# Down projection of a SwiGLU block on one Trainium2 core: 16 of its 44 feature tiles by Strassen pairs

## The chip, the cores and the metric

The kernel runs on one core of one Trainium2 chip. The metric is the device time of one execution in microseconds (us), as the median of several runs. A core has five engines that run their own instruction lists in order and wait for one another by semaphores: TensorE (PE in the profile; its weight loads are PEld), VectorE (DVE), ScalarE (ACT), GpSimd (POOL) and SyncE (SP). SP, ACT and POOL also issue DMA transfers, each on its own queue. The matmuls take float32 numbers split into a high and a low part, so that one exact-enough product is three matmuls: high by low, high by high, low by high.

## The reference, cut to what matters

```python
def reference(x, ..., ffn_pre_g, ffn_post_g, w_gate_up, w_down):
    ...                                   # attention and convolution give h (512 x 2048)
    u = rms_norm(h, ffn_pre_g[l])
    gate, up = jnp.split(u @ w_gate_up[l], 2, axis=-1)      # 2048 -> 2 x 5632
    f = (jax.nn.silu(gate) * up) @ w_down[l]                # 5632 -> 2048
    h = h + rms_norm(f, ffn_post_g[l])
    return h
```

There are 512 tokens. In tiles of 128, the hidden width 5632 is FT = 44 feature tiles and the model width 2048 is KT = 16 output tiles.

## The kernel before

All activations lie transposed: a tile is 128 features by 512 tokens. The part at issue is the last two stages.

*The f stage* makes the 44 activation tiles (gate times up) and stores each in DRAM, in `a_d`. Tiles 0 to 4 are made by plain matmuls. For the tiles 5 to 43, `strassen` (L206) takes the two weight tiles of gate and up (each 16 tiles of 128 by 128) as the two halves of a 2 x 2 block product with seven products instead of eight. Each call works on four "quarters" of 128 x 1024 weights, loaded by SP (`quarter`, L216), and on four sums of quarters. The first sum, `s1` (names `f20s`, and so on), is made by transfers: SP loads one quarter, then POOL issues a transfer that adds the other onto it (L250, L251). VectorE makes the other sums, `s2` to `s4` (L222, L267). For each product ACT rounds the weights to their high part (`h`, L232), VectorE subtracts for the low part (`l`, L234), and TensorE runs eight matmuls of 512 columns (L237) and eight of 256 (L239). Their right-hand operands are halves of the activations and sums of halves, prepared ahead by `winograd_t` (L192 to L195) and `merged` (L145): a tile with the high part in its left half and the low part in its right half.

*The down projection* is plain. It goes in two halves of FH = 22 feature tiles. In each half it goes over the 16 outputs in pairs. `gemm` (L159) takes the features in groups of eight. For each group and output it loads a weight chunk of 128 x 1024 (`wchunk`, L116: SP loads `raw_wd`, ACT rounds to `whi_wd`, VectorE subtracts to `wlo_wd`), and runs three matmuls of 512 columns per feature tile (L170, L173, L174). An activation tile comes back from `a_d` by `load` (L733): a POOL transfer into `ad`, then `split`, ACT for `fa..h` (L134) and VectorE for `fa..l` (L135). Of the first half three tiles are loaded before the last f calls (EARLY) and five behind them (MORE); the rest as the groups come up. The results of the first half stay in SBUF (`y`), and the second half is added to them by VectorE.

*The tail* is the norm of the result over features (`rstd`, `by_column`), the residual and the output, and the last two outputs are made in two halves of tokens (`products`).

The helper `rstd` adds up squares over features with matmuls by ones (`r_s`), scales the sum on VectorE (`r_v`, L292) and takes the power -0.5 on POOL (`r_r`, L294); `by_column` spreads the result over the partitions by matmuls with the identity (`r_b`, L301).

A scheduler orders the instructions of each engine when the program is built, by priorities from the order of the code; some places are pinned (`keep_in_program_order`). Buffers are rings: three each for high and low weights, six for raw weights, two for each kind of sum (tags `S` and `S1`), and 66 slots of 128 x 512 shared by everything called `slot`. A transfer into a ring's next buffer waits until that buffer's last reader is done.

Of the kernel before, what the change touches and what calls it, by code (L numbers as in the profile page):

```python
# [62 lines left out]
def hybrid_block(ctx: ExitStack, tc, xT, vecs, rpb, mask, w_c0, w_qk, w_v, w_gg, w_cg, w_ao, w_co, w_out, w_g0, w_gu, w_dn, outT):  # L63
# [51 lines left out]

    def wchunk(src, name, parts=1):  # L116
        w = src.shape[-1]
        raw = wp.tile([P, 1024], F32, tag="raw", name=f"raw_{name}", bufs=6)[:, :w]
        hi = wp.tile([P, 1024], F32R, tag="whi", name=f"whi_{name}")[:, :w]
        lo = wp.tile([P, 1024], F32R, tag="wlo", name=f"wlo_{name}")[:, :w]  # L120
        for n in range(parts):
            s = slice(n * w // parts, (n + 1) * w // parts)
            nc.sync.dma_start(raw[:, s], src[:, s])
            nc.scalar.copy(hi[:, s], raw[:, s])  # L124
            nc.vector.tensor_tensor(out=lo[:, s], in0=raw[:, s], in1=hi[:, s].bitcast(F32), op=ALU.subtract)  # L125
        taps(rate)
        return hi, lo
# [146 lines left out]
    def joined(out, c):  # L274
        nc.vector.tensor_tensor(out=out, in0=c[0], in1=c[1], op=ALU.add)  # L275

    def rstd(acc, n, name, blocks=range(NB), pin=False):

        ps = abank(f"{name}_s")
# [9 lines left out]
        nc.vector.tensor_scalar(out=v[:, bs], in0=ps[:, bs], scalar1=1.0 / n, scalar2=EPS, op0=ALU.mult, op1=ALU.add)  # L292
        r = const.tile([P, NB], F32, name=f"{name}_r")
        nc.gpsimd.tensor_tensor(out=r[:, bs], in0=v[:, bs], in1=mhalf[:, bs], op=ALU.pow)  # L294
# [442 lines left out]

    for j in range(5, FT):
# [12 lines left out]
        nc.scalar.dma_start(a_d[j], t)  # L751


    y = [None] * KT
    acc = None
    for half in range(2):
        for g in range(KT // 2):
            last = half == 0 and g == KT // 2 - 1
            if last:
                nxt = [load(FH + k) for k in range(EARLY)]  # L760
            if half == 1 and g == KT // 2 - 1:
                break
            outs = [((bank, abank)[g % 2](f"pd{half}_{o}"), o) for o in (2 * g, 2 * g + 1)]
            gemm([(ps, w_dn[half, o]) for ps, o in outs], acts, f"wd{half}_{g}", n=FH, more=lambda k: load(half * FH + k), pin=g < 2)
            if last:
                nxt += [load(FH + k) for k in range(EARLY, EARLY + MORE)]
            for ps, o in outs:
                if half == 0:
                    y[o] = slot(f"y{o}")
                    nc.scalar.copy(y[o], ps)  # L770
                else:
                    nc.vector.tensor_tensor(out=y[o], in0=ps, in1=y[o], op=ALU.add)
                    acc = sumsq(acc, y[o], f"y{o}")
                    nc.scalar.activation(y[o], y[o], AF.Copy, scale=col(C_FPOST, o))
        acts = nxt
# [5 lines left out]
    def products(n, between=()):  # L781
        cols = (A, B)[n]
        outs = [((bank, abank)[n](f"pl{n}_{o}"), o) for o in (KT - 2, KT - 1)]
        gemm([(ps[:, A], w_dn[1, o]) for ps, o in outs], acts, f"wl{n}", n=FH, cols=cols, between=between)
        for (ps, o), q in zip(outs, sq):
            nc.vector.tensor_tensor(out=y[o][:, cols], in0=ps[:, A], in1=y[o][:, cols], op=ALU.add)
            nc.scalar.activation(q[:, cols], y[o][:, cols], AF.Square)
# [127 lines left out]
```

## Time and profile before

| | |
|---|---|
| median of 3 runs | 2588.96 us (2587.96 to 2590.28) |
| the profiled execution's own time | 2587.58 us |
| its span, first to last instruction | 2585.8 us |
| mean granted TensorE clock | 0.991 |
| f stage by Strassen calls | to about 2058 us |
| plain down projection | about 2058 to 2560 us |
| tail | about 2560 to 2585.8 us |
| time from issue to landing of `raw_wd` (512 KB), `ad` (256 KB) | 3.5 and 4.8 us (medians) |

The profile is of one execution. A line "L237" is a line of the kernel before; in the changed kernel the same code stands some lines lower. A group's row gives the line, the engine, the operation, the names out<-in with their shapes, the count, the busy time in us and the mean of one in ns, then the idle time ahead of it and what ended that. Matmuls overlap, so the pace is the distance between their starts, not their duration.

### The profile page before, as it was taken

Reading aid. Unit: us, or ns where it says so; the run is one execution under the profiler, and the core shown is the slowest. Engines: PE = TensorE matmul, PEld = TensorE weight load, DVE = VectorE, ACT = ScalarE, POOL = GpSimd, SP = SyncE. Lnnn points to the kernel's source line nnn. Section 1 sums busy time; section 2 is a strip of 40 time slices with the busy share of each in tenths; the row PEclk is TensorE's granted clock in tenths of the full one; section 3 lists DMA queues with packets and bytes.
Section 4 is the critical chain, followed back from the end, with each engine's and each line's share of the span. In section 5 each row is a group of like instructions: output and inputs, shape, how many; then the busy total and the mean of one; then the engine's idle time right before and its main releaser. Section 6 shows DMA issues by size and latency. Waiting matters only on the chain.

```text
span 2585.8 us, 33614 instructions
## 1 busy us (share of the span) xinstructions
PE 2535.4 (98%) x13078; PEld 2168.7 (84%) x13078; DVE 1751.2 (68%) x2224; ACT 1079.6 (42%) x1560; POOL 263.9 (10%) x290
## 2 busy tenths in 40 slices
PE   9999999989999999998999999999999999999996
PEld 8888888778888888887998888888888878888886
DVE  5999896687776655338888888888788832233336
ACT  5223333455554422224555555555555532233222
POOL 0110222320000011004100000000000100010003
PEclk9999999989999999999999999999999999999998
DMA  6234323356667435234356656656655653353334
GB/s 215 93 127 148 108 95 104 109 149 189 184 189 251 143 129 189 95 104 151 107 158 182 173 172 180 179 171 173 185 169 168 206 174 103 94 170 98 96 97 136
DMA packets 124624, 385.42 MB, mean 149 GB/s; under 512 B 14256, under 2 KB 21552, under 8 KB 124464
## 3 DMA queue, kind: packets, MB, share of 16 engines
q1 hardware_dynamic: 96464, 311.47, 37.0%
q0 software_dynamic: 13024, 45.62, 8.7%
q10 hardware_dynamic: 14976, 26.19, 2.8%
q8 instruction: 102, 1.67, 0.3%
q14 instruction: 58, 0.48, 0.1%
HBM read 350.72 MB, written 32.51 MB: 148 GB/s over the span
## 4 chain that ended last, share of the span: by engine, by line
PE 92%; DVE 4%; issue 2%; ACT 1%; DMA 1%; POOL 1%; POOLq 0%; DVEq 0%; ACTq 0%; SPq 0%
PE f L237 19%; PE f L239 10%; PE g L237 7%; PE pd L170 5%; PE pd L173 5%; PE pd L174 5%; PE g L239 3%; PE po L173 2%; PE po L174 2%; PE po L170 2%; PE qk L174 2%; PE qk L173 2%; PE qk L170 2%; PE py L170 2%; PE py L174 2%; PE py L173 2%
## 5 line engine op out<-in xcount | busy, mean ns | idle before, releaser
L125 DVE TENSOR_TENSOR wlo_wd<-raw_wd,whi_wd 128x1024 fp32r<-128x1024 f32 (+1 forms) x90 | 102.3, 1136 | 283.7 <-ACT whi_wd L124 283.7
L124 ACT CAST whi_wd<-raw_wd 128x1024 fp32r<-128x1024 f32 (+1 forms) x90 | 88.4, 982 | 312.8 <-PE pd L173 306.8
L376 DVE SCALAR_TENSOR_TENSOR cv<-z,vec,cv 128x497 f32<-128x497 f32 (+14 forms) x240 | 190.9, 797 | 4.7
L125 DVE TENSOR_TENSOR wlo_wo<-raw_wo,whi_wo 128x1024 fp32r<-128x1024 f32 x36 | 47.4, 1318 | 106.9 <-ACT whi_wo L124 106.9
L124 ACT CAST whi_wo<-raw_wo 128x1024 fp32r<-128x1024 f32 x36 | 37.9, 1054 | 130.0 <-PE po L173 122.7
L124 ACT CAST whi_y<-raw_y 128x1024 fp32r<-128x1024 f32 x32 | 33.5, 1052 | 78.8 <-PE py L173 75.5
L124 ACT CAST whi_qk<-raw_qk 128x1024 fp32r<-128x1024 f32 x32 | 33.6, 1051 | 77.1 <-PE qk L173 52.7
L125 DVE TENSOR_TENSOR wlo_qk<-raw_qk,whi_qk 128x1024 fp32r<-128x1024 f32 x32 | 40.4, 1261 | 32.3 <-ACT whi_qk L124 32.1
L125 DVE TENSOR_TENSOR wlo_y<-raw_y,whi_y 128x1024 fp32r<-128x1024 f32 x32 | 52.2, 1634 | 10.7 <-ACT whi_y L124 9.5
L616 DVE TENSOR_TENSOR gg<-py,gg 128x512 f32<-128x512 f32 x32 | 21.8, 690 | 53.1 <-PE py L174 53.1
L294 POOL TENSOR_TENSOR r_r<-r_v,mhalf 128x2 f32<-128x2 f32 (+1 forms) x6 | 7.7, 1283 | 458.2 <-DVE r_v L292 458.2
L735 POOL DMA_DIRECT2D ad<-a_d x44 | 24.0, 555 | 262.4 <-PE pd L170 197.6
L170 PE MATMUL py<-ycl,whi_y 128*128 128x512 f32 x128 | 49.8, 389 | 0.0
L173 PE MATMUL py<-ych,whi_y 128*128 128x512 f32 x128 | 49.8, 389 | 0.0
L174 PE MATMUL py<-ych,wlo_y 128*128 128x512 f32 x128 | 49.8, 389 | 0.0
L747 ACT ACTIVATE sg<-sg 128x512 f32<-128x512 f32 x39 | 24.7, 634 | 50.2 <-DVE sg L275 50.2
L455 POOL TENSOR_TENSOR bm<-braw,msk 128x128 f32<-128x128 f32 x56 | 43.0, 801 | 14.0 <-DMA braw<-in_rpb 13.9
L153 PE MATMUL f<-b,whi_f 128*128 128x256 f32 x128 | 36.2, 283 | 0.0
L154 PE MATMUL f<-b,wlo_f 128*128 128x256 f32 x128 | 36.2, 283 | 0.0
L152 PE MATMUL f<-b,whi_f 128*128 128x256 f32 x128 | 36.2, 283 | 0.0
L626 POOL TENSOR_TENSOR gg<-gg,gg 128x512 f32<-128x512 f32 x16 | 21.7, 1355 | 111.2 <-ACT whi_y L124 69.6
L124 ACT CAST whi_ca<-raw_ca 128x1024 fp32r<-128x1024 f32 x12 | 12.6, 1053 | 47.2 <-PE cb L173 19.0
(3045 smaller groups left out, 8284.4 us busy)
## 6 DMA issues: line engine op xcount, KB each, us to landing
raw_wd<-in_w_dn SPq DMA_DIRECT2D x60, 512.0 KB, 3.5
raw_wo<-in_w_out SPq DMA_DIRECT2D x36, 512.0 KB, 3.8
raw_qk<-in_w_qk SPq DMA_DIRECT2D x32, 512.0 KB, 3.7
raw_wd<-in_w_dn SPq DMA_DIRECT2D x30, 384.0 KB, 3.1
a_d<-sg ACTq DMA_DIRECT2D x44, 256.0 KB, 3.7
ad<-a_d POOLq DMA_DIRECT2D x44, 256.0 KB, 4.8
raw_v<-in_w_v SPq DMA_DIRECT2D x16, 512.0 KB, 4.4
raw_y<-in_w_ao SPq DMA_DIRECT2D x16, 512.0 KB, 3.7
```

Of the source, the lines that this page charges most:

```text
L124: nc.scalar.copy(hi[:, s], raw[:, s])
L125: nc.vector.tensor_tensor(out=lo[:, s], in0=raw[:, s], in1=hi[:, s].bitcast(F32), op=ALU.subtract)
L152: nc.tensor.matmul(o, hi, t[:, B], start=first, stop=False, skip_group_check=True)
L153: nc.tensor.matmul(o, hi, t[:, A], start=False, stop=False, skip_group_check=True)
L154: nc.tensor.matmul(o, lo, t[:, A], start=False, stop=last, skip_group_check=True)
L170: mmul = nc.tensor.matmul(ps, hi[:, s], al, start=first, stop=False)
L173: nc.tensor.matmul(ps, hi[:, s], ah, start=False, stop=False)
L174: nc.tensor.matmul(ps, lo[:, s], ah, start=False, stop=last)
L237: nc.tensor.matmul(ps, hi[:, ws[k]], t, start=first and k == 0, stop=False, skip_group_check=True)
L239: nc.tensor.matmul(ps[:, A], lo[:, ws[k]], t[:, A], start=False, stop=last and k == HT - 1, skip_group_check=True)
L376: nc.vector.scalar_tensor_tensor(out=a[:, to], in0=z[:, fr], scalar=col(C_WDW, i * CW + w), in1=a[:, to], op0=ALU.mult, op1=ALU.add)
L455: nc.gpsimd.tensor_tensor(out=bm[:, o + i - i0], in0=raw[:, :, i * BC : (i + 1) * BC], in1=msk[:, o + i - i0, None, :].broadcast_to([P, RO ...
```

## The change

The down projection is cut into three parts: features 0 to 3 (DN_F = 4) plainly, 4 to 19 (16 tiles) by Strassen calls over pairs of outputs, and 20 to 43 (24 tiles) plainly. The parts of one output are added up in DRAM, in `y_d`: the first part is written there by ACT's queue, the second is added by POOL transfers that accumulate, and the sum is loaded by SP and added to the third part.

The 16 middle tiles are scaled by token before they are split: the squares of tiles 4 to 19 are summed over features (`activated`: ACT squares, POOL adds into `asum`); after f21 `rstd` and `by_column` give the row `ra` and its inverse `ia`; then POOL loads each of the 16 tiles, multiplies it by the row and stores it in `as_d` (`scaled`, during f22 to f37). In the first plain part, SP loads pairs of these (`da`, 512 KB) and VectorE and ACT make the Strassen operands (`prepare`). The results of the Strassen calls are multiplied by the inverse row `irow` on POOL (`ys`) before they are added to `y_d`.

The raw ring goes from six to five buffers. The weight layout for the down projection is the plain one for all 44 tiles.

```diff
+DN_F = 4
+DN_S = DN_F + KT
+DN_R = FT - DN_S
-        raw = wp.tile([P, 1024], F32, tag="raw", name=f"raw_{name}", bufs=6)[:, :w]
+        raw = wp.tile([P, 1024], F32, tag="raw", name=f"raw_{name}", bufs=5)[:, :w]
+    def winograd_tt(un, tt):
+        left = un.rearrange("p k (h t) -> p (k h) t", h=2)
+        nc.vector.tensor_tensor(out=tt[:, :, A], in0=left[:, 1::2], in1=left[:, 0:2], op=ALU.subtract)
+        nc.vector.tensor_tensor(out=tt[:, 0, B], in0=un[:, 1, B], in1=tt[:, 0, A], op=ALU.subtract)
+        nc.vector.tensor_tensor(out=tt[:, 1, B], in0=un[:, 1, A], in1=tt[:, 0, B], op=ALU.subtract)
+    def activated(j, t):
+        nc.scalar.dma_start(a_d[j], t)
+        if j == DN_F:
+            nc.scalar.activation(asum, t, AF.Square)
+        elif DN_F < j < DN_S:
+            sq = slot(f"asq{j}")
+            nc.scalar.activation(sq, t, AF.Square)
+            nc.gpsimd.tensor_tensor(out=asum, in0=asum, in1=sq, op=ALU.add)
+    def scaled(k):
+        t = slot(f"an{k}")
+        nc.gpsimd.dma_start(t, a_d[DN_F + k])
+        nc.gpsimd.tensor_tensor(out=t, in0=t, in1=arow, op=ALU.mult)
+        nc.gpsimd.dma_start(as_d[k], t)
...
         c11, c12, c21, c22 = strassen(w_gu[j], w_gu[FT + j], op, f"f{j}", j)
-        if j == FT - 1:
-            acts += [load(k) for k in range(EARLY, EARLY + MORE)]
+        if j == DN_S + 1:
+            ra, va = rstd([asum], KT * P, "ra", eps=TINY)
+            nc.scalar.copy(arow, by_column(ra, "ra"))
+            ia = const.tile([P, NB], F32, name="ia")
+            nc.vector.tensor_tensor(out=ia, in0=va, in1=ra, op=ALU.mult)
+            nc.scalar.copy(irow, by_column(ia, "ia"))
+        if DN_S + 2 <= j < DN_S + 2 + KT:
+            scaled(j - DN_S - 2)
...
+    def prepare(c):
+        un = stp.tile([P, 2, NT], F32, tag="S1", name=f"da{c}")
+        load_in_order(un, as_d[c : c + HT + 1 : HT].rearrange("k p t -> p k t"))
+        b11.append(merged(un[:, 0, A], f"d11_{c}"))
+        b2.append([merged(un[:, 1, cols], f"d2{c}_{n}") for n, cols in enumerate((A, B))])
+        tt = stp.tile([P, 2, NT], F32, tag="S", name=f"dt{c}")
+        winograd_tt(un, tt)
+        ...
+    acts += [load(k) for k in range(EARLY, DN_F)]
+    for o in range(KT):
+        ps = (bank, abank)[o % 2](f"pd0_{o}")
+        gemm([(ps, w_dn[o])], acts, f"wd0_{o}", n=DN_F, pin=o < 2)
+        t = stp.tile([P, NT], F32, tag="quad", name=f"yf{o}", bufs=3)
+        nc.scalar.copy(t, ps)
+        nc.scalar.dma_start(y_d[o], t)
+        if o % 2 == 0:
+            prepare(o // 2)
+    op = operands(b11, b2, b_t12, b_t34)
+    for o in range(0, KT, 2):
+        if o == KT - 2:
+            acts = [load(DN_S + k) for k in range(EARLY)]
+        w0, w1 = (w_dn[o + i, :, DN_F * P : DN_S * P] for i in range(2))
+        c11, c12, c21, c22 = strassen(w0, w1, op, f"d{o}", o // 2)
+        for i, (ca, cb) in enumerate(((c11, c12), (c21, c22))):
+            t = slot(f"ys{o + i}")
+            joined(t[:, A], ca)
+            joined(t[:, B], cb)
+            nc.gpsimd.tensor_tensor(out=t, in0=t, in1=irow, op=ALU.mult)
+            nc.gpsimd.dma_start(y_d[o + i], t, accum_op=ALU.add)
+    acts += [load(DN_S + k) for k in range(EARLY, EARLY + MORE)]
-    for half in range(2):
-        for g in range(KT // 2):
-            ...
+    for g in range(KT // 2 - 1):
+        outs = [((bank, abank)[g % 2](f"pd1_{o}"), o) for o in (2 * g, 2 * g + 1)]
+        for _, o in outs:
+            y[o] = slot(f"y{o}")
+            load_in_order(y[o], y_d[o])
+        gemm([(ps, w_dn[o, :, DN_S * P :]) for ps, o in outs], acts, f"wd1_{g}", n=DN_R, more=lambda k: load(DN_S + k), pin=g < 2)
...
```

Three places of the instruction lists show what it moves. The first is TensorE between the calls f21 and f22 (`t_1`, `b_0` are right-hand operands; a number behind a name is a buffer's). Before:

```order
L239 MATMUL f_1_13939<-t_1_10895,f21l 128x256
L239 MATMUL f_1_13939<-t_1_10950,f21l 128x256
L239 MATMUL f_1_13939<-t_1_10999,f21l 128x256
L237 MATMUL f_0_14121<-b_0_10321,f22h 128x512
L237 MATMUL f_0_14121<-b_0_10352,f22h 128x512
L237 MATMUL f_0_14121<-b_0_10389,f22h 128x512
```

and after:

```order
L250 MATMUL f_1_13989<-t_1_10999,f21l 128x256
L296 MATMUL ra_s<-ones,asum 128x1 x4
L248 MATMUL f_0_14194<-b_0_10321,f22h 128x512
L248 MATMUL f_0_14194<-b_0_10352,f22h 128x512
L312 MATMUL ra_b<-ident,ra_r 128x128 x4
L312 MATMUL ia_b<-ident,ia 128x128 x4
L248 MATMUL f_0_14194<-b_0_10389,f22h 128x512
```

The sums of squares, and behind two matmuls of f22 the spreading of both rows, now stand in TensorE's list at this place.

The second is VectorE in the plain down projection, where it prepares the weights of the outputs ahead of TensorE. Before, in the first half, it holds weight chunks alone:

```order
L125 TENSOR_TENSOR wlo_wd_3_0_8_18865<-raw_wd_3_0_8_18863,whi_wd_3_0_8_18864 128x1024
L125 TENSOR_TENSOR wlo_wd_3_1_8_18895<-raw_wd_3_1_8_18893,whi_wd_3_1_8_18894 128x1024
L125 TENSOR_TENSOR wlo_wd_3_0_16_18925<-raw_wd_3_0_16_18923,whi_wd_3_0_16_18924 128x768
L125 TENSOR_TENSOR wlo_wd_3_1_16_18949<-raw_wd_3_1_16_18947,whi_wd_3_1_16_18948 128x768
L125 TENSOR_TENSOR wlo_wd_4_0_0_18979<-raw_wd_4_0_0_18977,whi_wd_4_0_0_18978 128x1024
```

and after, at the end of the 4-tile part (`wlo_wd_15` belongs to its last output, `d0s` with two inputs is `s2` of the first Strassen call d0, `d0q` its quarters; `d_0`, `d_1` are operands from `dt`):

```order
L151 TENSOR_TENSOR d_1_18845<-dt_18838,d_1_18845 128x256
L151 TENSOR_TENSOR d_0_18848<-dt_18838,d_0_18848 128x256
L233 TENSOR_TENSOR d0s_18910<-d0s_18879,d0q 128x1024
L151 TENSOR_TENSOR d_1_18851<-dt_18838,d_1_18851 128x256
L129 TENSOR_TENSOR wlo_wd_15_0_0_18857<-raw_wd_15_0_0_18855,whi_wd_15_0_0_18856 128x512
L233 TENSOR_TENSOR d0s_18957<-d0q 128x1024
L245 TENSOR_TENSOR d0l<-d0q,d0h 128x1024
```

VectorE's list now mixes operands, sums of d0 and weights, and `s2` of d0 stands ahead of the low part of the last plain output's weights. The buffers `da` and `d0s_18879` are of the ring `S1`.

The third is POOL where the last part begins. Before, at the first half's start, loads of activations (`ad`) alternate with early loads for the tail (`ha`):

```order
L735 DMA ad_17793<-a_d 128x512
L735 DMA ad_18156<-a_d 128x512
L735 DMA ad_18162<-a_d 128x512
L800 DMA ha_21067<-h_d 128x4x256
L735 DMA ad_18168<-a_d 128x512
L804 DMA ha_21071<-h_d 128x2x256
L800 DMA ha_21069<-h_d 128x4x256
L735 DMA ad_18174<-a_d 128x512
```

and after, at the 24-tile part's start (`ys_20356`, `ys_20361` are the two results of the last Strassen call, d14; `ad_20176` is the third activation of the part, `ad_20366` the fourth):

```order
L758 DMA ad_20176<-a_d 128x512
L873 DMA ha_21874<-h_d 128x4x256
L877 DMA ha_21878<-h_d 128x2x256
L829 TENSOR_TENSOR ys_20356<-ys_20356,irow 128x512
L830 DMA y_d<-ys_20356 128x512
L758 DMA ad_20366<-a_d 128x512
L829 TENSOR_TENSOR ys_20361<-ys_20361,irow 128x512
L830 DMA y_d<-ys_20361 128x512
L758 DMA ad_20372<-a_d 128x512
```

The fourth and fifth loads now stand behind the two products of the last call and their accumulating transfers.

More of the change, by code (lines that the diff above doesn't have):

```diff
@@ L47 @@
 EPS = 1e-6
+TINY = 1e-30
 SCALE = P ** -0.5
-FH = FT // 2
+DN_F = 4
+DN_S = DN_F + KT
+DN_R = FT - DN_S
 LN_AT = 8
@@ L215, in quarter @@
         def quarter(w, c):
-            raw = wp.tile([P, 1024], F32, tag="raw", name=f"{name}q", bufs=6)
+            raw = wp.tile([P, 1024], F32, tag="raw", name=f"{name}q", bufs=5)
             nc.sync.dma_start(raw, w[:, c * 1024 : (c + 1) * 1024])
@@ L275, in joined, with rstd @@
         nc.vector.tensor_tensor(out=out, in0=c[0], in1=c[1], op=ALU.add)
-    def rstd(acc, n, name, blocks=range(NB), pin=False):
+    def rstd(acc, n, name, blocks=range(NB), pin=False, eps=None):
         ps = abank(f"{name}_s")
@@ L291, in rstd @@
         v = const.tile([P, NB], F32, name=f"{name}_v")
-        nc.vector.tensor_scalar(out=v[:, bs], in0=ps[:, bs], scalar1=1.0 / n, scalar2=EPS, op0=ALU.mult, op1=ALU.add)
+        nc.vector.tensor_scalar(out=v[:, bs], in0=ps[:, bs], scalar1=1.0 / n, scalar2=eps or EPS, op0=ALU.mult, op1=ALU.add)
         r = const.tile([P, NB], F32, name=f"{name}_r")
         nc.gpsimd.tensor_tensor(out=r[:, bs], in0=v[:, bs], in1=mhalf[:, bs], op=ALU.pow)
-        return r
+        return (r, v) if eps else r
     def by_column(r, name, blocks=range(NB), pin=False):
@@ L341, in x_pair @@
     def x_pair(c, name):
-        x2 = wp.tile([P, 1024], F32, tag="raw", name=name, bufs=6)
+        x2 = wp.tile([P, 1024], F32, tag="raw", name=name, bufs=5)
         if c or name != "x0":
@@ L723, in hybrid_block @@
                 b_t34.append([merged(t34[:, cols], f"t34{i}_{n}") for n, cols in enumerate((A, B))])
+    asum = const.tile([P, NT], F32, name="asum")
+    def activated(j, t):
[6 more added lines that the diff above has]
+            nc.gpsimd.tensor_tensor(out=asum, in0=asum, in1=sq, op=ALU.add)
     for j in range(2):
@@ L727, in hybrid_block @@
         nc.vector.tensor_tensor(out=t, in0=pf[2 * j + 1], in1=t, op=ALU.mult)
-        nc.scalar.dma_start(a_d[3 + j], t)
+        activated(3 + j, t)
     op = operands(b11, b2, b_t12, b_t34)
@@ L736, in load @@
         return split(t, f"fa{k}")
+    as_d = dr.tile([KT, P, NT], F32, name="as_d")
+    y_d = dr.tile([KT, P, NT], F32, name="y_d")
+    arow, irow = asum, const.tile([P, NT], F32, name="irow")
+    def scaled(k):
[3 more added lines that the diff above has]
+        nc.gpsimd.dma_start(as_d[k], t)
     for j in range(5, FT):
@@ L750, in hybrid_block @@
         nc.vector.tensor_tensor(out=t, in0=t, in1=up, op=ALU.mult)
-        nc.scalar.dma_start(a_d[j], t)
+        activated(j, t)
+    b11, b2, b_t12, b_t34 = [], [], [], []
+    def prepare(c):
[5 more added lines that the diff above has]
+        winograd_tt(un, tt)
+        b_t12.append([merged(tt[:, 0, cols], f"d12{c}_{n}") for n, cols in enumerate((A, B))])
+        b_t34.append([merged(tt[:, 1, cols], f"d34{c}_{n}") for n, cols in enumerate((A, B))])
@@ L754, in hybrid_block @@
+    acts += [load(DN_S + k) for k in range(EARLY, EARLY + MORE)]
     y = [None] * KT
     acc = None
-    for half in range(2):
-        for g in range(KT // 2):
[L758 to L775, printed above, removed]
+    for g in range(KT // 2 - 1):
[4 more added lines that the diff above has]
+        gemm([(ps, w_dn[o, :, DN_S * P :]) for ps, o in outs], acts, f"wd1_{g}", n=DN_R, more=lambda k: load(DN_S + k), pin=g < 2)
+        for ps, o in outs:
+            nc.vector.tensor_tensor(out=y[o], in0=ps, in1=y[o], op=ALU.add)
+            acc = sumsq(acc, y[o], f"y{o}")
+            nc.scalar.activation(y[o], y[o], AF.Copy, scale=col(C_FPOST, o))
@@ L778, in hybrid_block @@
+    for o in (KT - 2, KT - 1):
+        y[o] = slot(f"y{o}")
+        load_in_order(y[o], y_d[o])
     sq = [slot(f"sq{o}") for o in (KT - 2, KT - 1)]
@@ L783, in products @@
         outs = [((bank, abank)[n](f"pl{n}_{o}"), o) for o in (KT - 2, KT - 1)]
-        gemm([(ps[:, A], w_dn[1, o]) for ps, o in outs], acts, f"wl{n}", n=FH, cols=cols, between=between)
+        gemm([(ps[:, A], w_dn[o, :, DN_S * P :]) for ps, o in outs], acts, f"wl{n}", n=DN_R, cols=cols, between=between)
         for (ps, o), q in zip(outs, sq):
@@ L825, in hybrid_block @@
     for i, k in ((0, 4), (4, 4), (8, 4), (12, 2), (14, 2)):
-        o = wp.tile([P, 4, HN], F32, tag="raw", name=f"o{i}", bufs=6)
+        o = wp.tile([P, 4, HN], F32, tag="raw", name=f"o{i}", bufs=5)
         for m in range(i, i + k):
@@ L892, in _layout @@
         w_gu=tiles(w_gate_up[0]),
-        w_dn=c(w_down[0].reshape(2, FH, P, KT, P).transpose(0, 3, 2, 1, 4).reshape(2, KT, P, FH * P)),
+        w_dn=tiles(w_down[0]),
     )
```

## The prediction

> **What bounds the kernel now.** The page's first and fourth parts come first, because they say which engine a change must relieve.
>
> ```profile
> PE 2535.4 (98%) x13078; PEld 2168.7 (84%) x13078; DVE 1751.2 (68%) x2224; ACT 1079.6 (42%) x1560; POOL 263.9 (10%) x290
> PE 92%; DVE 4%; issue 2%; ACT 1%; DMA 1%; POOL 1%; POOLq 0%; DVEq 0%; ACTq 0%; SPq 0%
> ```
>
> TensorE is busy 98% of the span and carries 92% of the chain that ended last. So a matmul saved is time saved, and a wait added on TensorE is time lost in full. What a stage costs comes from TensorE's timeline (start, duration) and from a view by windows (window, its length, busy time of PE, PEld, DVE, ACT, POOL with counts, granted clock, DMA share, GB/s).
>
> ```profile
> 1621.21 1.09 PE L237 MATMUL f<-b,f21h 128*128 128x512 f32 x4
> 1640.77 1.55 PE L237 MATMUL f<-b,f22h 128*128 128x512 f32 x6
> 1621.21:1640.77 19.56, 19.56 (x115) 17.20 (x114) 15.81 (x19) 10.26 (x15) 0.87 (x1) 1.00 0.62 172
> 2400.00:2500.00 100.00, 100.00 (x443) 82.81 (x442) 33.25 (x36) 29.98 (x37) 0.00 (x0) 1.00 0.35 102
> ```
>
> The first two rows are the starts of neighbouring Strassen calls: one takes 19.56 us for two outputs by 16 tiles, with VectorE busy 15.81 us of it. The last row is the plain down projection: 443 matmuls touch the stretch, about 441 start in it, so one takes 0.2267 us and 96 (two outputs, 16 tiles, three each) take 21.75.
>
> TensorE's waits (waited for, total, times, longest) name the stalls left in the down projection:
>
> ```profile
> PE pd L170 <- DVE fa18l L135: 1.4, 1, 1.4
> PE pd L170 <- DVE fa40l L135: 1.4, 1, 1.4
> PE pd L170 <- DVE fa11l L135: 0.3, 1, 0.3
> PE pd L170 <- DVE fa33l L135: 0.3, 1, 0.3
> ```
>
> Each half pays for its start: one activation split is late in the second group of eight tiles, one in the third. Waits count from the modelled end of the matmul ahead (some 0.39 us long, at a pace of 0.227), so TensorE loses 0.16 more at each: 4.0 us in all.
>
> **The terms.** U is the end of a stage on TensorE, T its start.
>
> *Matmuls.* Eight pairs of outputs go from 21.75 to 19.56 us over 16 tiles: 8 x 2.19 = **-17.5**. The 4 and the 24 plain tiles cost per tile what they did. The stalls of the two half starts go: **-4.0**; what is late in their stead is the fourth term.
>
> *The norm's rows (ra, ia), once, between f21 and f22.* The nearest rows are the layer norm's, with the same steps:
>
> ```profile
> 868.72 1.03 PE L285 MATMUL rc_s<-ones,cv_sq 128*128 128x1 f32 x8
> 869.62 0.49 PE L170 MATMUL py<-ya0l,whi_y 128*128 128x512 f32 x1
> 869.79 0.16 DVE L292 TENSOR_SCALAR rc_v<-rc_s 128x4 f32<-128x4 f32 x1 [0.99 <-PE rc_s L285]
> 870.04 1.96 POOL L294 TENSOR_TENSOR rc_r<-rc_v,mhalf 128x4 f32<-128x4 f32 x1 [60.75 <-DVE rc_v L292]
> 872.06 1.16 PE L301 MATMUL rc_b<-ident,rc_r 128*128 128x128 f32 x8 [1.02 <-POOL rc_r L294]
> 872.97 0.48 PE L174 MATMUL py<-ya1h,wlo_y 128*128 128x512 f32 x1
> ```
>
> Eight `rc_s` take 0.90 us to the next start, so four `ra_s` take 0.45. From the last sum's start (869.51) to `rc_b` it is 2.55 us. TensorE has only two matmuls of f22 in between (0.45 us), so it idles 2.0; `ra_b` and `ia_b` cost 0.91 each, as `rc_b` does, and `ia` itself is done under `ra_b`. 0.45 + 2.0 + 1.8 = **+4.2**; from 3.5 (a shorter power on POOL) to 5.5 (`ra_v` one 1.2 us step later on VectorE).
>
> *From the 4 plain tiles into the first Strassen call.* The stage has 16 x 12 matmuls, 43.5 us. In it VectorE makes the Strassen operands too, and in its fixed order `s2` of d0 stands ahead of `wlo_wd_15`, which TensorE needs at T + 15 x 2.72 + 0.45 = T + 41.25. `s2` waits for POOL's accumulate into `d0s`, that for SP's load of it, and that for the buffer that `da6` leaves. Rows (KB and median us to landing of f20's two and of a weight chunk; then min/median/max to landing of every first-term load on SP and of every accumulate on POOL; then VectorE):
>
> ```profile
> f20s<-in_w_gu SPq DMA_DIRECT2D x1, 512.0 KB, 4.1
> f20s<-in_w_gu POOLq DMA_DIRECT2D x1, 512.0 KB, 6.2
> raw_wd<-in_w_dn SPq DMA_DIRECT2D x60, 512.0 KB, 3.5
> DMA to landing us min/median/max: 3.7/4.1/7.0
> DMA to landing us min/median/max: 5.6/6.3/9.0
> 1639.44 0.42 DVE L275 TENSOR_TENSOR sg<-f,f21c 128x256 f32<-128x256 f32 x1
> 1639.78 1.21 DVE L267 TENSOR_TENSOR f22s<-f22q,f22s 128x1024 f32<-128x1024 f32 x1
> 2083.61 0.69 DVE L135 TENSOR_TENSOR fa11l<-ad,fa11h 128x512 fp32r<-128x512 f32 x1
> 2084.21 0.68 DVE L135 TENSOR_TENSOR fa12l<-ad,fa12h 128x512 fp32r<-128x512 f32 x1
> ```
>
> By start-to-start VectorE takes 0.34 us for 256 columns and 0.60 for 512; nine and three of them make 4.9 us per pair of plain outputs, beside 5.44 on TensorE, and each `da` (512 KB, taken as 4.1 too) can start only when the one two before it has been read. Followed in order with these times, `da6` is read by about T + 38 (T + 34 if every `da` is there at once). Then 4.1 + 0.1 (semaphore to POOL, an estimate from the 0.25 between `rc_v` and `rc_r`) + 6.3 + 1.2 (`s2`) + 0.34 + 0.60: `wlo_15` is done at T + 50.6. Stall **+9.3**. Queued behind the waiting `s2` on VectorE are only d0's own steps, which TensorE wants later than `wlo_15`. Lower end: T + 34 and the shortest landings (3.7, 5.6): +4.2. Upper: `da` loads of 5.0 and a slower accumulate: +14.
>
> *From the last Strassen call into the 24 plain tiles.* Three activations are ready at U, enough for nine matmuls, 2.04 us. The fourth load stands on POOL behind `ys14 * irow` and its accumulate.
>
> ```profile
> ad<-a_d POOLq DMA_DIRECT2D x44, 256.0 KB, 4.8
> DMA to landing us min/median/max: 2.8/4.8/11.5
> L626 POOL TENSOR_TENSOR gg<-gg,gg 128x512 f32<-128x512 f32 x16 | 21.7, 1355 | 111.2 <-ACT whi_y L124 69.6
> 2082.60 0.62 ACT L134 CAST fa11h<-ad 128x512 fp32r<-128x512 f32 x1
> ```
>
> The product into c12 ends 2.8 us (one product) before U; copy and two joins bring it to U - 1.5, POOL's product (1.36, L626) to U - 0.2, the accumulate's issue to about U + 0.6. The load issued then lands 5.8 us later (above the median 4.8: the first weight chunks load beside it), and the split takes 1.7 (fa11's cast from 2082.60 to the end of its low part at 2084.30): U + 8.1, against U + 2.04, a stall of 6.1. The fifth load waits on POOL for `ys15` too: another 2.2. Then the two later groups of eight are late as each half start was (2.0), and a cast of the next weights ahead of `fa29h` on ACT doubles that: 3.9. Sum **+12.2**; lower end 5.6 (landing in 2.8, later groups 2.0), upper 16 (landing in 9).
>
> *TensorE's clock after a stall.* The start of the feed-forward stage shows it, and the tail:
>
> ```profile
> 1210.00:1212.00 2.00, 1.43 (x7) 0.85 (x5) 2.00 (x2) 1.12 (x2) 1.80 (x2) 1.00 0.23 78
> 1212.00:1214.00 2.00, 0.51 (x1) 0.19 (x1) 2.00 (x2) 0.00 (x0) 1.85 (x1) 1.00 0.07 16
> 1214.00:1216.00 2.00, 1.54 (x4) 1.26 (x5) 2.00 (x4) 0.96 (x2) 0.00 (x0) 0.51 0.79 268
> 1216.00:1218.00 2.00, 2.00 (x7) 1.61 (x6) 2.00 (x3) 1.22 (x2) 1.57 (x1) 0.63 0.30 113
> 2562.34 0.59 PE L285 MATMUL r_s<-ones,sq 128*128 128x1 f32 x2 [2.38 <-ACT sq L787]
> 2564.00:2566.00 2.00, 1.86 (x8) 1.78 (x8) 0.00 (x0) 0.59 (x2) 0.00 (x0) 0.50 0.40 132
> ```
>
> From 1211.4 to 1214.4 TensorE ran one matmul; then the granted clock was about 0.5 until some 1217.3, which loses 1.4 us. I take 1.4 for the 9.3 us stall, 1.0 after the 6.1 one (part of it falls into the wait for the next activation) and 0.4 for the norm's 2.0 us idle, which may or may not do it (2.38 did in the tail, 1.02 before `rc_b` did not): **+2.8**, between 0 and 4.5.
>
> The Trainium skill, "TensorE: Matmul & The Clock Gate", section "Part 1: The HAM clock gate", says that TensorE drops to half clock after an idle window of about 3.4 us and returns after as long a busy one. By it the two long stalls would cost 1.7 each and the norm nothing, 3.4 in place of 2.8 and the sum 0.6 higher. The trace agrees on the half clock, and has it after shorter idle time.
>
> *Costed at nothing.* Squares (ACT), their sums and the `scaled` products (POOL, 1.36 each) in the f stage: ACT is busy 10.26 of 19.56 us, POOL 0.87, and VectorE's idle 3.75 us per call cover what POOL slows; should that cover go, see the last rival. Five raw buffers for six: loads take 3.5 to 5 us and are still issued some ten ahead. `y_d` writes and reads: done a stage before they are needed, on queues that have room at a DMA share of 0.35. In the tail one square waits for a buffer: **+0.3**.
>
> Sum: -17.5 - 4.0 + 4.2 + 9.3 + 12.2 + 2.8 + 0.3 = **+7.3 us**. The profiled execution took 2587.58 us (span 2585.8 and 1.8 around it), so 2594.9; it was 1.4 below the median 2588.96, from which it would be 2596.3. I say **2596**.
>
> **Rivals.** "No change" means within 0.2% (5.2 us, about what a measurement here can tell): 2583.8 to 2594.1.
>
> 1. *Every load lands at its shortest*, since the queues are half empty there: the two stage starts cost 4.2 and 5.6, the clock nothing: -17.5 - 4.0 + 4.2 + 4.2 + 5.6 + 0.3 = -7.2, **2582**, faster. It decides once the two starts and the clock cost less than 11.8 together. For it: DMA share 0.35 in the plain stage. Against: 0.62 beside Strassen calls, and a first group of `ad` loads that went up to 11.5. Chance 0.13.
> 2. *Two thirds of the waits*: `da` landing in 3.6 (T + 36, +7), one late activation less (+8), clock 1.4: -0.6, **2588**, no change. For it: raw chunks of 512 KB land in 3.5 by the median. Chance 0.27.
> 3. *Loads in each other's way*: +14 and +16, clock 4: +17, **2606**. For it: maxima of 7.0, 9.0 and 11.5. Against: medians near the minima. Chance 0.14.
> 4. *VectorE becomes the bound of the Strassen stages*, held up by POOL:
>
> ```profile
> L125 DVE TENSOR_TENSOR wlo_y<-raw_y,whi_y 128x1024 fp32r<-128x1024 f32 x32 | 52.2, 1634 | 10.7 <-ACT whi_y L124 9.5
> L125 DVE TENSOR_TENSOR wlo_wd<-raw_wd,whi_wd 128x1024 fp32r<-128x1024 f32 x60 | 73.5, 1225 | 165.6 <-ACT whi_wd L124 165.6
> ```
>
> Beside POOL's `gg` sums the same subtraction took 1.63 in place of 1.23. One 1.36 us product per call (two in the down calls) leaves 15.8 + 2.7 = 18.5 of 19.56, so it decides only where it hits the 3.75 us of slack at a bad place; 0.5 us in each of 24 calls gives 12 more, **2608**. Chance 0.04. The Trainium skill, "GPSIMD Engine Reference", section "Specifications", says that POOL shares its path to SBUF with VectorE, in contention with two-input operations; the rows agree.
>
> That the Strassen calls don't run at 19.56 at all finds no support: they are the same function on the same sizes.
>
> **The numbers.** My sum has 0.42, with 2592 to 2601 as its own range, 0.06 of it below 2594.1. Slower: 0.36 + 0.14 + 0.04 = 0.54; no change 0.06 + 0.27 = 0.33; faster 0.13. The range for 8 in 10 cuts half of rival 1 and the upper end of 3 and 4: 2582 to 2605.
>
> **What the next profile would show.** Windows: Strassen pairs of the down stage at 19.56 us, else the first term is wrong. TensorE's waits: `ra_b` on POOL near 1.6; a `wd` matmul on `wlo_wd` near 9, the last of the 16 plain outputs; `fa23l` near 6 and `fa24l` near 2; granted clock near 0.5 for about 3 us behind the two long ones. I am wrong if `d0s` lands before T + 39, if `fa23l` is there at U + 4, or if VectorE has no idle time left in f22 to f37.

## The result and the profile after

The changed kernel takes 2606.4 us (median of 4, 2605.21 to 2607.76) against 2588.46 for the kernel before on the same chip: a ratio of 1.0071, 95% interval 1.0058 to 1.0083. It is slower, as forecast, but by 18 us and not by 7, and just above the range of 2582 to 2605. The profiled execution's span is 2604.7 us, 18.9 above the 2585.8 of before; the ledger below is of these two.

The page's parts 1 and 4 of the changed kernel, and TensorE's waits in the two last stages (waited for, total, times, longest):

```profile
PE 2529.2 (97%) x13242; PEld 2169.2 (83%) x13242; DVE 1889.2 (73%) x2394; ACT 1142.3 (44%) x1690; POOL 369.6 (14%) x378
PE 70%; DVE 3%; issue 2%; DMA 2%; POOL 1%; ACT 1%; DVEq 0%; POOLq 0%; ACTq 0%; SPq 0%
PE pd L178 <- DVE wlo_wd L129: 13.5, 5, 8.7
PE pd L174 <- DVE fa23l L139: 11.1, 1, 11.1
PE pd L174 <- DVE fa29l L139: 2.1, 1, 2.1
PE pd L174 <- DVE fa38l L139: 1.4, 1, 1.4
PE ra_b L312 <- POOL ra_r L305: 0.8, 1, 0.8
PE d L248 <- ACT d14v L238: 0.8, 1, 0.8
```

TensorE is busy 6 us less and the span is 19 longer. The longest waits are the ones named ahead: the last plain output's `wlo_wd` (8.7 of the 13.5), `fa23l`, one split late in each later group. The other four waits on `wlo_wd`, 4.8 us on earlier outputs of the 4-tile part, were not named. The windows of the changed kernel, cut at the first matmul of f21, f24, the plain part, d2, d14, the last pair of outputs, and at the end (columns as before):

```profile
1619.48:1681.89 62.41, 61.61 (x362) 54.23 (x361) 48.98 (x57) 31.93 (x45) 12.14 (x13) 1.00 0.64 190
2072.96:2156.08 83.12, 69.62 (x306) 55.74 (x305) 57.03 (x111) 46.79 (x101) 3.47 (x4) 0.92 0.76 230
2156.08:2273.65 117.57, 117.57 (x674) 103.31 (x673) 102.07 (x103) 57.93 (x79) 37.38 (x31) 1.00 0.73 184
2273.65:2541.96 268.31, 252.65 (x1123) 208.34 (x1121) 96.77 (x107) 82.54 (x107) 25.64 (x36) 0.97 0.46 138
2541.96:2604.69 62.73, 39.93 (x321) 39.17 (x319) 41.02 (x62) 15.85 (x22) 20.29 (x22) 0.84 0.47 150
```

and the corresponding two of the kernel before, its whole down projection to the last pair, and the tail:

```profile
2070.94:2524.36 453.42, 450.02 (x1983) 371.31 (x1981) 141.54 (x155) 131.39 (x171) 14.50 (x27) 1.00 0.39 117
2524.36:2585.80 61.44, 37.64 (x297) 36.89 (x295) 39.82 (x62) 15.01 (x22) 20.66 (x22) 0.81 0.44 140
```

With 0.2267 us per matmul and 19.56 per Strassen call, matmuls alone would fill 58.7, 63.1, 117.4 and 248.1 us of the first four. So f21 to f24 loses 3.7 us, the first stage start 20.0, the calls d2 to d12 nothing (0.2), the last stage start with d14 20.2. The last four rows come to 531.7 us against 514.9 for the two of before, +16.9; the norm's rows +3.7; the stages ahead of f5 were 1.7 shorter in this execution (they vary by some 4 us over the profiles below): 18.9.

**The first stage start.** The plain part's first matmul is at T = 2072.96. VectorE, SP and TensorE of the changed kernel (start, duration, idle before and what ended it); the last two rows are VectorE's wait for all `da` (from the plain part's first matmul to d0's) and min/median/max to landing of d0's two first-sum transfers:

```profile
2105.67 0.69 DVE L204 TENSOR_TENSOR dt<-da 128x512 f32<-128x512 f32 x1 [3.26 <-DMA da<-as_d]
2106.28 0.42 DVE L151 TENSOR_TENSOR d<-da,d 128x256 fp32r<-128x256 f32 x1
2106.95 0.75 DVE L151 TENSOR_TENSOR d<-da,d 128x256 fp32r<-128x256 f32 x2
2107.73 0.38 SPq L91 DMA_DIRECT2D da<-as_d  x1
2114.64 0.33 SPq L261 DMA_DIRECT2D d0s<-in_w_dn  x1
2129.22 1.23 DVE L233 TENSOR_TENSOR d0s<-d0s,d0q 128x1024 f32<-128x1024 f32 x1 [8.05 <-DMA d0s<-in_w_dn]
2130.70 0.69 DVE L129 TENSOR_TENSOR wlo_wd<-raw_wd,whi_wd 128x512 fp32r<-128x512 f32 x1
2131.44 0.80 PE L178 MATMUL pd<-fa0h,wlo_wd 128*128 128x512 f32 x1 [8.71 <-DVE wlo_wd L129]
2132.03 0.63 PE L174 MATMUL pd<-fa1l,whi_wd 128*128 128x512 f32 x1
2132.46 0.63 PE L177 MATMUL pd<-fa1h,whi_wd 128*128 128x512 f32 x1
DVE dt L204 <- DMA da<-as_d: 10.9, 6, 3.3
DMA to landing us min/median/max: 5.5/7.0/8.5
```

The chain is the forecast one, link by link: `da` late at every pair, then `d0s` loaded once `da6` has been read, `s2` behind it, `wlo_15` behind `s2`. Why `da` is late shows in the rows at 2105.67 to 2107.73. VectorE's `dt` step, which waits for `da6` to land, stands in its list ahead of the last three `d` steps from a `da`; SP issues the next load 0.03 us after these end (by the ring of two they read the tile before). So no two of these loads are under way at once: from `da3` on, and for `d0s`, each was issued 1.9 to 2.8 us after the one before it had landed.

After the wait TensorE's starts are 0.43 us apart in place of 0.227: half clock.

**The last stage start**, on ScalarE, VectorE and POOL (the stage begins at U = 2294.26):

```profile
2290.76 0.62 ACT L138 CAST fa22h<-ad 128x512 fp32r<-128x512 f32 x1 [2.84 <-issue]
2291.29 1.05 ACT L128 CAST whi_wd<-raw_wd 128x1024 fp32r<-128x1024 f32 x1
2292.24 0.36 ACT L256 COPY d14c<-d 128x256 f32<-128x256 f32 x1
2295.31 0.41 DVE L286 TENSOR_TENSOR ys<-d,d14c 128x256 f32<-128x256 f32 x1
2295.88 2.10 POOL L829 TENSOR_TENSOR ys<-ys,irow 128x512 f32<-128x512 f32 x1 [6.52 <-DVE ys L286]
2298.89 0.89 POOL L758 DMA_DIRECT2D ad<-a_d  x1
2306.15 0.62 ACT L138 CAST fa23h<-ad 128x512 fp32r<-128x512 f32 x1 [11.12 <-DMA ad<-a_d]
```

The copy `d14c` stands behind `fa22h`, whose load was issued at 2283.55 and landed at 2290.69. The fourth activation's load is issued at U + 4.6, and is there 7.2 us later.

### The profile page after: what moved, and what is told of

Read it like the earlier page. It is cut to its first block, busy times and chain, and to the rows that moved or that the text cites. A ratio compares the mean times of both kernels' runs of the same rounds, so it can differ in the third digit from the quotient of the medians.

```text
span 2604.7 us, 34628 instructions
## 1 busy us (share of the span) xinstructions
PE 2529.2 (97%) x13242; PEld 2169.2 (83%) x13242; DVE 1889.2 (73%) x2394; ACT 1142.3 (44%) x1690; POOL 369.6 (14%) x378
## 4 chain that ended last, share of the span: by engine, by line
PE 70%; DVE 3%; issue 2%; DMA 2%; POOL 1%; ACT 1%; DVEq 0%; POOLq 0%; ACTq 0%; SPq 0%
PE f L248 19%; PE f L250 10%; PE g L248 7%; PE g L250 4%; PE pd L174 3%; PE pd L177 3%; PE pd L178 3%; PE d L248 3%; PE po L174 2%; PE po L177 2%; PE po L178 2%; PE py L174 2%; PE py L178 2%; PE py L177 2%; PE d L250 1%
## 5 line engine op out<-in xcount | busy, mean ns | idle before, releaser
L129 DVE TENSOR_TENSOR wlo_wd<-raw_wd,whi_wd 128x1024 fp32r<-128x1024 f32 (+1 forms) x58 | 62.1, 1075 | 111.4 <-ACT whi_wd L128 109.6
L128 ACT CAST whi_wd<-raw_wd 128x1024 fp32r<-128x1024 f32 (+1 forms) x58 | 53.9, 934 | 154.2 <-PE pd L177 151.0
L745 POOL TENSOR_TENSOR asum<-asum,asq 128x512 f32<-128x512 f32 x15 | 20.1, 1343 | 243.6 <-ACT asq L744 243.6
L829 POOL TENSOR_TENSOR ys<-ys,irow 128x512 f32<-128x512 f32 x16 | 29.1, 1820 | 84.1 <-DVE ys L286 53.7
L769 POOL TENSOR_TENSOR an<-an,asum 128x512 f32<-128x512 f32 x16 | 25.6, 1600 | 103.9 <-DMA an<-a_d 101.9
L843 DVE TENSOR_TENSOR y<-pd,y 128x512 f32<-128x512 f32 x14 | 9.7, 691 | 41.5 <-PE pd L178 41.5
```

What stands on the lines that cost most here:

```text
L769: nc.gpsimd.tensor_tensor(out=t, in0=t, in1=arow, op=ALU.mult)
L829: nc.gpsimd.tensor_tensor(out=t, in0=t, in1=irow, op=ALU.mult)
```

## The experiments

Theory A: instruction queues that are served in order, and rings of two buffers, put a transfer behind work that finishes late. Rival B: the transfers are crowded there, and late in any order. The table gives the median, the ratio to the kernel before with its interval, and TensorE's time in the windows above, from each variant's profile.

| kernel | us | ratio | f21-f24 | plain4 to d2 | d2-d14 | d14 to last pair |
|---|---|---|---|---|---|---|
| matmuls alone | | | 58.7 | 63.1 | 117.4 | 248.1 |
| the change | 2606.4 | 1.0071 (1.0058-1.0083) | 62.4 | 83.1 | 117.6 | 268.3 |
| e1 loads first | 2598.9 | 1.0048 (1.0033-1.0063) | 62.4 | 81.6 | 117.6 | 262.8 |
| e2 da in the raw ring | 2597.5 | 1.0041 (1.0026-1.0056) | 62.4 | 68.7 | 117.6 | 269.1 |
| e3 s1 of d0 in the raw ring | 2606.5 | 1.0074 (1.0059-1.0089) | 62.4 | 80.0 | 117.6 | 268.2 |
| e5 e1 + e2 + rows later | 2588.0 | 0.9999 (0.9990-1.0009) | 61.3 | 69.3 | 117.6 | 262.1 |
| e6 da alternating | 2601.2 | 1.0050 (1.0036-1.0064) | 62.4 | 73.7 | 117.6 | 268.3 |
| e7 16 loads first, ha last | 2592.6 | 1.0014 (1.0005-1.0023) | 61.3 | 74.7 | 118.2 | 258.1 |
| e7 without ha last | 2593.4 | 1.0018 (1.0009-1.0027) | 61.3 | 76.2 | 118.8 | 261.0 |
| e8 24 loads first, shared chunk | 2577.7 | 0.9962 (0.9949-0.9974) | 61.3 | 71.2 | 118.3 | 252.0 |
| e9 24 loads first | 2578.4 | 0.9963 (0.9949-0.9976) | 61.3 | 68.9 | 118.7 | 252.3 |

### e1: the activations ahead of the last products

```diff
         c11, c12, c21, c22 = strassen(w0, w1, op, f"d{o}", o // 2)
+        if o == KT - 2:
+            acts += [load(DN_S + k) for k in range(EARLY, EARLY + MORE)]
...
-    acts += [load(DN_S + k) for k in range(EARLY, EARLY + MORE)]
```

> Against the changed kernel (2606.4 us): the loads of the 4th to 8th activation of the 24-tile part are issued on POOL ahead of the two products of the last Strassen call, with nothing else changed and the same bytes moved. Theory A (a queue in order: the load stood behind products that waited for the joins, and was issued 4.6 us after the Strassen stage's end): the 11.1 us wait for fa23l falls under 2 us and the half clock behind it goes, so 11 to 13 us come back: 2593 to 2595 us, with the wait on wlo_wd (8.7) at the other stage start unchanged. Rival B (the DMA engines are full there, a share of 0.94 to 1.02, and the load takes as long whenever it is issued): a wait of 6 us or more stays, on fa23l or on an activation behind it, and less than 5 us come back: 2601 us or more.

Measured: the median falls by 7.5 us and the window by 5.5, less than theory A's 11 to 13. The wait for `fa23l` is gone, and another has come, on the first activation of the next group (TensorE's waits, then POOL):

```profile
PE pd L174 <- DVE fa28l L139: 4.5, 1, 4.5
PE pd L174 <- DVE fa24l L139: 0.8, 1, 0.8
2302.86 1.34 POOL L831 TENSOR_TENSOR ys<-ys,irow 128x512 f32<-128x512 f32 x1 [9.01 <-PE pd L174]
2307.15 0.89 POOL L758 DMA_DIRECT2D ad<-a_d  x1
```

The next group's first load (2307.15) now stands behind the products, which are later still, since VectorE does the new splits before the joins. The same loads, issued earlier, no longer hold TensorE up at `fa23l`, so their place in the queue was the cause there, as A says; A's number missed that the wait would pass on to the next load in it.

### e2 and e3: the buffers of da, and of d0's first sum

```diff
-        un = stp.tile([P, 2, NT], F32, tag="S1", name=f"da{c}")
+        un = wp.tile([P, 1024], F32, tag="raw", name=f"da{c}", bufs=5).rearrange("p (k t) -> p k t", t=NT)
```

> The operand loads da take buffers of the raw ring (five deep) in place of the two of ring S1; d0s finds S1 free and is loaded before the 4-tile part begins. Same bytes. Theory A (a ring of two makes each da load wait for the reading of the one two before it, and d0s wait for da6): TensorE's stage of 62.9 us for 43.5 us of matmuls shrinks to 43.5 to 46, all waits on wlo_wd in it fall under 1.5 us, and 17 to 19 us come back: 2587 to 2590 us. Rival B (VectorE has too much work there, or the transfers are too slow for any order): the waits on wlo_wd add up to 6 us or more and less than 12 come back: 2594 us or more.

The window falls from 83.1 to 68.7, 14.4 us of the 20 it lost; the clock stays at 1.00. By the median 9 us come back, half of the 17 to 19 that A expected (the waits on `wlo_wd` are in A's range, the total in B's); in this profile 10.8 do, as the stages ahead of f21 took 2.4 us longer and the other end 0.8:

```profile
2075.38:2144.06 68.68, 65.24 (x306) 52.70 (x305) 57.46 (x112) 46.62 (x101) 1.68 (x2) 1.00 0.78 255
PE pd L178 <- DVE wlo_wd L129: 3.4, 6, 1.0
```

Transfers passed there at 255 GB/s against 230, so the change's stage was not limited by their rate. The gain did not come the way that was expected. The `da` loads were hardly earlier: the last landed at T + 38.3 against T + 38.9, for SP now waited before them for buffers of the raw ring. Its waits for `da` loads (L91), in the change and in e2:

```profile
SPq L91 <- DVE d L151: 13.6, 5, 5.1
SPq L91 <- DVE wlo_wd L129: 18.3, 5, 4.2
```

What moved is `d0s`. It was issued a stage earlier, at 2038.26, the sum was in place 27 us ahead of T, and VectorE's 8.0 us wait for it is gone, with the half clock behind it. e3 puts only d0's `s1` into the raw ring and leaves `da` in S1:

```diff
-        s1 = stp.tile([P, 1024], F32, tag="S1", name=f"{name}s1")
+        s1 = wp.tile([P, 1024], F32, tag="raw", name=f"{name}s1", bufs=5) if name == "d0" else stp.tile(...)
```

> Only d0's first sum s1 takes a buffer of the raw ring; da keeps the two of S1. This takes away the last link alone, d0s waiting for da6 to be read. Theory A: d0s is loaded right behind da7, some 6 us earlier, the longest wait on wlo_wd falls from 8.7 to 1 to 3 us, while the small ones before it (13.5 less 8.7, 4.8 us, by VectorE waiting for da) stay: 6 to 9 us come back, 2597 to 2600 us. Rival C (the da loads alone are behind all of it, s1 would have been late anyway): 8.7 stays above 5 and less than 4 come back, 2602 us or more.

Only 3.1 us of the window come back, and the total does not move. VectorE still waits 6.6 us for the accumulate:

```profile
DVE d0s L233 <- DMA d0s<-in_w_dn: 6.6, 1, 6.6
PE pd L178 <- DVE wlo_wd L129: 9.9, 7, 5.2
```

SP issues `d0s` behind `da7` in its list, at 2108.95 in place of 2114.64, and the accumulate, beside three of d0's quarters and d2's first sum, lands in 9.1 us in place of 8.5. So it is there 5.7 us earlier after T. But the scheduler also gave VectorE another order: behind `s2` now stand six operand steps and d0's next sum, 3.2 us, ahead of `wlo_15`:

```profile
2123.34 1.23 DVE L233 TENSOR_TENSOR d0s<-d0s,d0q 128x1024 f32<-128x1024 f32 x1 [6.60 <-DMA d0s<-in_w_dn]
2124.48 0.75 DVE L151 TENSOR_TENSOR d<-da,d 128x256 fp32r<-128x256 f32 x2
2125.15 1.43 DVE L151 TENSOR_TENSOR d<-dt,d 128x256 fp32r<-128x256 f32 x4
2126.61 1.22 DVE L233 TENSOR_TENSOR d0s<-d0q 128x1024 f32<-128x1024 f32 x1
2127.75 0.68 DVE L129 TENSOR_TENSOR wlo_wd<-raw_wd,whi_wd 128x512 fp32r<-128x512 f32 x1
```

So e3 did not take away the last link alone. A's number failed and C's held, but not C's reason: in e2 the `da` loads are as late, and the long wait is gone. In e2 the accumulate landed in 5.6 us.

### e5: both ends, and the norm's rows one call later

```diff
             ra, va = rstd([asum], KT * P, "ra", eps=TINY)
+        if j == DN_S + 2:
             nc.scalar.copy(arow, by_column(ra, "ra"))
...
-        if DN_S + 2 <= j < DN_S + 2 + KT:
-            scaled(j - DN_S - 2)
+        if DN_S + 3 <= j < DN_S + 3 + KT:
+            scaled(j - DN_S - 3)
```

> Loads first and da in the raw ring together, and the spreading of the norm's two rows one Strassen call later (after f22 in place of f21), so that TensorE does not wait for POOL's power between. Theory A: the parts add up, -12 - 18 - 1 = -31, 2575 us, 0.5 per cent below the kernel before: the 17.6 us of saved matmuls show, less 3 for the norm's rows, less late activations in the two later groups of eight. Rival B: the same transfers squeezed into less time collide, waits come up at other places and the time stays above 2584 us.

The windows add up: 21.1 us against 5.5 + 14.4 + 1.1 of the parts (the median moves by 18.4), and the time is that of the kernel before. The expected 31 failed with the two numbers it was made of. B's bound on the time holds, but its reason does not: no wait came up that the parts did not have (the longest here is 4.0 us, on `fa28l`).

### e6, e7: more depth, and more loads first

e6 takes S1 for even `da` and the raw ring for odd ones; e7 adds the rows, 16 activations loaded ahead of the last products, the first three of them a call earlier, and `ha` pinned behind them:

```diff
+            acts += [load(DN_S + k) for k in range(EARLY, 16)]
...
-        nc.gpsimd.dma_start(t, h_d[...])
+        tc.keep_in_program_order(nc.gpsimd.dma_start(t, h_d[...]))
```

> The operand loads da alternate between ring S1 and the raw ring, nothing else is changed against the changed kernel; so both rings hold prefetched tiles and d0s waits for da4 only. Theory A (the waits that were left with da in the raw ring alone, 1.0 to 1.5 us of VectorE at each da, came from the raw ring's depth): TensorE's time from the first matmul of the 4-tile part to d2, 83.1 us changed and 68.7 with the raw ring alone, against 63.1 of matmuls, falls to 63.5 to 66; the total is 2588 to 2592. Rival B (the transfers are too slow there at a DMA share of 0.74 to 0.78, whatever the ring): it stays at 68 to 70, the total at 2594 to 2598.

> da alternating; rows spread one call later; the first three activations of the 24-tile part loaded one Strassen call earlier, the next thirteen ahead of the last call's products, and the early loads for the tail (ha, 2 MB) moved on POOL behind all activations. Theory A (what is left at the last stage start in the version with all fixes so far, 4.0 + 2.0 + 2.0 + 1.4 us, is again loads that stand on POOL behind products, and a load behind ha transfers that wait for buffers): the time from d14 to the last pair, 262.1 there, 248.1 of matmuls, falls to 249 to 253, and with 4 us from the first start the total is 2571 to 2576 us, a ratio of 0.994 to 0.996 to the kernel before. Rival B (DMA crowding): activations late elsewhere, ScalarE's in-order casts holding up the copies of d14, the total 2580 or more.

> As the run before, but the ha loads stay where the scheduler puts them, among the activation loads of the last Strassen call. If their 2 MB and their waits for buffers at the head of POOL's queue matter: 2 to 4 us above the run before. If they do not: within 1 us of it.

e6 is worse than e2 (73.7 against 68.7), against both theories' numbers: with `da` in S1 again, `d0s` is loaded inside the stage once more (SP 2098.29; accumulate 8.1 us to landing), and TensorE's longest wait on `wlo_wd` is 3.4. Together with e2 this says that most of e2's gain came from `d0s` being loaded ahead of the stage; that alone, with `da` left in S1, was not run. e7 inherits e6's loss (74.7), so its total, 2592.6, is above e5's and misses A's 2571 to 2576; its other end, 258.1, misses A's 249 to 253 too, though it is 4.1 us better than e5's, and 2.9 better than without moving `ha`. In the total that move is worth 0.8 us, within the noise: by the expectation it does not matter. At that end the wait has moved to the third group:

```profile
PE pd L174 <- DVE fa36l L139: 3.6, 1, 3.6
```

whose first load again stands behind the last products.

### e8 and e9: nothing behind the last products

```diff
+            acts += [load(DN_S + k) for k in range(EARLY, 24)]
```

Both keep e2's `da`, the rows later and `ha` last; e8 also loads the first three activations two calls ahead, and one 512 KB weight chunk for two outputs in the 4-tile part.

> da in the raw ring; in the 4-tile part the weights of two outputs come as one 512 KB chunk (one raw buffer and one cast and subtraction in place of two, so five buffers hold two and a half pairs of outputs); rows spread one call later; in the last part all 24 activations are loaded ahead of the products of the last Strassen call, which nothing needs before the tail, the first three by transfers two calls ahead; the tail's ha loads behind them. Theory A (in-order queues and short rings made the lost time, so it is won back where nothing stands behind a late wait): first matmul of the 4-tile part to d2 64 to 66 us (69.3 with da in the raw ring, 63.1 of matmuls), d14 to the last pair 249 to 252 (262.1 and 258.1 before; 248.1 of matmuls), total 2570 to 2575 us, ratio 0.9935 to 0.9955. Rival B (crowded transfers, 6 MB of activations loaded at once beside the weights): d14 to the last pair 256 or more, total 2579 or more.

> As the run before without the shared weight chunk, and with the three early activations loaded and split one call ahead: tells the two ends apart. Theory A: pd to d2 stays at 68.5 to 70 us (as with da in the raw ring), d14 to the last pair within 2 us of the run before, so 4 to 6 us slower than it. Rival: pd to d2 within 1.5 us of the run before, the chunks were not what VectorE waited for.

Both are faster than the kernel before, by 0.38% and 0.37%. The window of d14 is 252 us, at the edge of A's 249 to 252; 21 activations of 256 KB loaded in one go cost TensorE two waits of 0.9 and 1.6 us between starts and no more. The shared chunk did not help: the first window is 71.2 us against 68.9, where A said 64 to 66 for e8. e8's total missed A's 2570 to 2575, and e9 is 0.7 us slower than e8, not 4 to 6. VectorE waits for `da` in both (e8, then e9):

```profile
DVE dt L204 <- DMA da<-as_d: 10.7, 4, 3.7
DVE dt L204 <- DMA da<-as_d: 6.9, 6, 1.3
```

so what is left in that stage is `da` itself. In e9, as in e2, SP waits 18 us before these loads for VectorE's `wlo_wd`, which frees raw buffers, and the last lands at T + 38.1. Neither ring made them earlier; which of SP's order, VectorE's order and the landing time sets them was not separated.

## Why the prediction was right in kind and wrong in size

- *Matmuls, -17.5*: right. d2 to d14 took 117.57 us for six calls, 19.6 each.
- *Old half starts, -4.0*: right to 0.5 (453.4 against 448.9 of matmuls), and the later groups of the last part cost 2.26 + 1.58 between starts, 3.8 where 3.9 was forecast.
- *The norm's rows, +4.2*: 3.7. The power took 1.03 us in place of 1.96, and the four sums 0.81 in place of 0.45. The forecast halved the 0.90 of eight `rc_s`, but a row counts each of these matmuls twice: the four `ra_s` of the list are x8 here:

```profile
1639.03 0.95 PE L296 MATMUL ra_s<-ones,asum 128*128 128x1 f32 x8
1639.84 0.71 PE L248 MATMUL f<-b,f22h 128*128 128x512 f32 x2
1640.26 1.03 POOL L305 TENSOR_TENSOR ra_r<-ra_v,mhalf 128x4 f32<-128x4 f32 x1 [12.69 <-DVE ra_v L303]
```

- *First stage start, +9.3 and 1.4 of clock*: 20.0. The step that failed is "`da6` is read by about T + 38" with what follows it. The forecast let each `da` start when the one two before it had been read; they went one at a time, in 3.4 to 6.0 us each. So `d0s` was issued at 2114.64, T + 41.7; its load took 5.5 in place of 4.1, the accumulate 8.5 in place of 6.3. `wlo_15` was done at T + 58.4, not T + 50.6. These 7.8 us, and 2.8 of half clock behind the wait in place of 1.4, are the difference. That the wait itself (8.7) is near the forecast 9.3 is luck: TensorE came to this matmul late as well, at T + 49.6 and not T + 41.25. Four outputs before had waited for `wlo_wd`, 5.8 us by TensorE's starts with half clock behind one of them, which the sum put at nothing. These waits lie inside the 58.4 and do not come on top of it.
- *Last stage start, +12.2 and 1.0*: 20.2. The step that failed is "copy and two joins bring it to U - 1.5". The copy stood on ScalarE behind `fa22h`, which waited for its load, and a weight cast; one join stood on VectorE behind two weight subtractions. So `ys14` was ready at U + 1.5, POOL's product took 2.1, and the load 7.2 in place of 5.8: `fa23l` cost 11.2 between starts in place of 6.1. The fifth load cost 0.7 in place of 2.2. A further 1.0 is in d14 itself, 20.6 us long, with a wait of 0.8 for ScalarE's copy `d14v` that the sum did not have.
- *Clock, +2.8*: by the starts that are 0.43 apart in place of 0.227, some 4.4 us at the first stage start and 3.0 at the last, 7.4 in all, of which 1.6 fall ahead of the wait for `wlo_15` and cost nothing more. Four waits were followed by it and not two, the shortest of them 2.1 us of idle time (`fa29l`).
- *At nothing*: the squares and `scaled` cost nothing, f24 to the plain part took 391.07 us in both kernels. In the tail the forecast 0.3 was -1.6: the window grew by 1.3 us with 24 more matmuls of 256 columns in it, 2.9 us at 0.12. The cause of that stays open.

Of the rivals the third, loads in each other's way, gave the right total (2606), but for half of the reason, so its number was partly luck: landings were longer, while the order and the buffers, not the transfers' rate, decided, as e2 and e9 show. Rival 4 did not come up: the six calls took 19.6 us each.

The Trainium skill ("TensorE: Matmul & The Clock Gate", "Part 1: The HAM clock gate") asks for an idle window of about 3.4 us before the half clock. Here idle times of 2.1 and 2.7 us were followed by it at once, so the trace differs on the length; 0.8 us before `ra_b` and 1.4 before `fa38l` were not. In e1 (2112.27) and e8 (2110.79) 2.5 us were not either, so between 2 and 3 us the length alone does not decide it.

## What to carry to other kernels

A matmul saving of 0.7% is lost at its two edges if the first transfers of the next stage stand in an in-order queue behind the results of the stage before; write the results last, when nobody needs them soon (e9). When a chain of waits is followed on paper, go by the list of the engine that frees the buffers: the steps that free one may stand behind a wait for the next load, and a ring of two then works like a ring of one. Take landing times from the crowded part of the trace. Removing one link of such a chain (e1, e3) can move the wait to the next one, and a rebuilt program may have another order (e3); judge a fix by the whole window, and look for which transfer it moved (e2).

## What the runs showed of the hardware

Behind the 8.7 us wait of the changed kernel twelve matmuls started 0.43 us apart, behind the 2.7 us wait (2110.03) six. The accumulating transfer of d0's first sum (512 KB) landed in 5.6 to 5.7 us where it was issued ahead of the 4-tile part (e2, e5, e8, e9), and in 7.6 to 9.4 inside it, beside other loads of 512 KB (the change, e1, e3, e6, both e7). POOL's product `ys` of 512 columns took 1.3 to 2.3 us.
